# Far scores as one product of 256 columns, and weight splitting kept off GpSimd's copies

## The chip, the core and the metric

The kernel runs on one core of a Trainium2 chip. A core has five engines with instruction streams of their own: TensorE (PE, matrix products; its weight loads are shown as PEld), VectorE (DVE), ScalarE (ACT), GpSimd (POOL) and SyncE (SP, which issues the DMAs here). They share an on-chip memory of 128 partitions (SBUF); PE writes its products to a second, small memory (PSUM) of eight banks of 512 fp32 columns. The metric is the device time of one execution in microseconds, the median of the runs.

## The reference, cut to what matters

One block of a conformer: an input projection, a gated causal convolution branch, an attention branch, a merge by gates, and a feed-forward part. 1024 tokens, width 1024, 16 heads of 64. The attention is the sum of three dilated windows, mixed by their log-sum-exp:

```python
DILATION_GROUPS = ((128, 1), (512, 4), (2048, 16))
...
    scores = jnp.einsum('nbqhd,nbkhd->nbhqk', qb, kc)
...
    scores = scores - slopes[:, None, None] * dist
    scores = jnp.where(valid[None, :, None], scores, -jnp.inf)
    m = jnp.max(scores, axis=-1, keepdims=True)
    p = jnp.exp(scores - m)
...
        mix = jax.nn.softmax(jnp.stack(lses), axis=0)
        o = jnp.einsum('gbsh,gbshd->bshd', mix, jnp.stack(outs))
```

A softmax over three windows mixed by log-sum-exp is one softmax over the union, in which a key that lies in several windows counts as often. The kernel computes that: the mask holds the logarithm of the count less the slope times the distance.

## The kernel before, in words

All products are made with fp32r operands, each fp32 number split into a high part (rounded, `hi`) and a low part (`lo`, the rest). A product of two split operands is three matmuls: high by high, high by low, low by high. The splitting is work for ACT (the rounded copy) and DVE (`lo = src - hi`).

The attention loop (L1104 on) is written out by hand for ACT, DVE, PE and POOL: within `tc.manual_schedule` the instructions of these engines keep the order of the program. SP's DMAs are put in order by a planner. The loop has 128 slots, 8 places for each of the 16 heads, and 13 slots more in which the work still under way runs out (`BACK` = 12). For each head, places 0 to 3 score the query tiles 3, 2, 1, 0 of the first half of the tokens (128 queries against the keys up to them); place 4 scores `far`, the second half's queries against the first half's keys by residues of the position modulo 4; places 5 to 7 score the query tiles 7, 6, and 4 with 5 against the near keys.

A slot does this, in this order:

- `score` (L931): the products of queries and keys into PSUM, then on DVE `least` (L925), which adds the mask and takes the least of the negated sum. The queries are one operand with high and low part on alternating partitions; the keys come as `kh` and `kl`, and two products (L922 and L923) are added up in PSUM.
- `share` (L969), in places 1 to 4, for the unit scored one slot before: DVE's reciprocal, and on POOL the multiplication `times` (L967).
- `piece_high(2)` (L186), if more than two pieces wait in the deque: ACT rounds one half of a weight tile or of an activation tile (L190). The pieces belong to the filler products.
- `fill(front)`: filler, that is so many steps of the generator `side_steps`, each three matmuls of 512 columns (L118 to L120) of the gate projection or of the convolution's output projection. They are independent of the attention, and keep PE at work while the attention's chain passes through the other engines.
- `by_residue` (L917), in places 7, 0 and 1 (`COPIES`): on POOL, copies of the queries, of `kh` and of `kl` of the next or the present head into `fars`, ordered by residue.
- `flip` (L1006), for what was scored twelve slots ago: transposes on PE (into `pp`), the high part on ACT (`ph`, L1034) and the low part on DVE (`pl`, L1035). In places 0 to 3 this is the second half of the tokens, far, (4), (5) and (6, 7, 3); in places 4 to 6 the first half.
- `weigh` (L1040), for what was flipped one slot ago: the products with the values, first with `ph`, then with `pl`.
- `result`, `compare`, `combine`: in place 5 `compare` and in place 6 `combine` (L993) compute what share of the softmax the far and the near part of a query has. `combine` has POOL multiply eight tiles: four of `far`, then those of the tiles 7, 6, 4, 5.
- `powers` (L963): ACT's exponential of the unit scored in this slot.
- `o_step` (L1079), in the last slots: a sum, a rounded copy and a subtraction on the attention's output, for the projection that follows.
- `piece_low` (L180): the subtraction on DVE (L183) for what `piece_high` has rounded.
- `fill(behind)`, and `piece_high(2)` once more.

`FRONT` and `BEHIND` say how many filler steps stand in each place; the first four slots have one more each (`START`).

PSUM: the pool `psA` has two tiles of two banks (`big_ps`), `psB` four of one bank (`bank_ps`). The scores use one bank each; a tile of `psA` is taken for two scores in turn (`score_banks`). Ahead of the attention, `psA` holds the last gate products (`gx`), which are copied out at L880.

Of the kernel before, what the change touches and what calls it, by code (L numbers as in the profile page):

```python
# [21 lines left out]
P = 128  # L22
# [12 lines left out]
WARM = 7  # L35
FRONT = (1, 1, 1, 1, 0, 1, 1, 1)
BEHIND = (1, 0, 0, 0, 1, 0, 1, 0)
BACK = 12
COPIES = (-1, 0, 1)
START = (1, 1, 1, 1, 0, 0, 0, 0, 0, 0, 0, 0)  # L40
TAIL = (1, 1)
# [18 lines left out]
def block_kernel(ctx: ExitStack, tc: tile.TileContext, x, xT, x0, g2, pack, mask,  # L60
# [10 lines left out]
    def big_ps(name):  # L71
        return psA.tile([P, T], F32, tag="A", name=name)
# [823 lines left out]
    if True:  # L896
# [17 lines left out]

        fars = p2b.tile([P, 3, 512], F32R, name="fars")

        def by_residue(h, n):  # L917
            t = tiles[h][0][:, 512:] if n == 0 else tiles[h][n][:, 0:512]
            pool.tensor_copy(fars[:, n].rearrange("p (r j) -> p r j", r=4), t.rearrange("p (j r) -> p r j", r=4))

# [10 lines left out]
        def score(h, tiles, units):  # L931
            q, kh, kl, m = tiles
            made = []
            if not score_banks:
                pair = big_ps(f"s_{h}_{units[0]}")
                score_banks.extend((pair[:, 512:], pair[:, :512]))
            s = score_banks.pop()
            tag, size = ("pf", 512) if units == ("far",) else ("p" + "".join(map(str, units)),
                                                            sum((i + 1 - lowest(i)) * P for i in units))
            whole = ready2(tag, [P, size], F32, 2, f"{tag}_{h}")  # L940
            if units == ("far",):
                for r in range(4):
                    scored(s[:, r * P : (r + 1) * P], *(fars[:, n, r * P : (r + 1) * P] for n in range(3)))
                for r in range(4):
                    pt = whole[:, r * P : (r + 1) * P]
                    pts[h, "far", r] = pt, own[h][:, 1, r]
                    least(pt, s[:, r * P : (r + 1) * P], m[:, 512:640], own[h][:, 1, r, 0:1])
                    made.append(pts[h, "far", r])
                return made
            at = 0  # L950
            for i in units:
                ks = slice(lowest(i) * P, (i + 1) * P)
                c = slice(at, at + ks.stop - ks.start)
                at = c.stop
                scored(s[:, c], q[:, i * P : (i + 1) * P], kh[:, ks], kl[:, ks])
                st = own[h][:, 0, i - 4] if i > 3 else ready2("st", [P, 8], F32, 4, f"st_{h}_{i}")
                pts[h, i] = whole[:, c], st
                made.append((s[:, c], m[:, 512 - c.stop + c.start : 512], *pts[h, i]))
            for sc, mc, pt, st in made:
                least(pt, sc, mc, st[:, 0:1])  # L960
            return [u[2:] for u in made]

        def powers(pt, st):  # L963
# [136 lines left out]
        ENG = mybir.EngineType  # L1100
        with tc.manual_schedule(engines={ENG.Activation, ENG.DVE, ENG.PE, ENG.Pool}):
            pend = []
            fill(1)
            for at in range(len(slots) + BACK + 1):  # L1104
# [14 lines left out]
                for unit in late:  # L1119
                    share(*unit)  # L1120
                if len(pieces) > 2:
                    piece_high(2)
# [26 lines left out]
                if at == len(slots):  # L1149
# [3 lines left out]
                    heads = [o_fetch(0, k) for k in range(0, KT - 2, 2)]  # L1153
                if at > len(slots) + 3:
                    o_step(heads)
                if at == len(slots) + BACK - 4:
                    heads.append(o_fetch(0, KT - 2))
                piece_low()
                fill(behind)
                piece_high(2)  # L1160
            for _ in gates:
# [627 lines left out]
```

## Time and profile before

| | us |
|---|---|
| median of 3 runs | 1702.61 (1701.63 to 1704.5) |
| profiled execution, its own time | 1701.83 |
| span of its trace | 1699.4 |
| PE busy | 1685.3 (99%) |
| DVE busy | 1298.0 (76%) |
| ACT busy | 785.8 (46%) |
| POOL busy | 226.5 (13%) |

How to read the rows: in an answer of the timeline, the columns are the start in us from the start of the span, the duration in us, the engine, the line, the operation, output and inputs by the program's names, and the shape with the number of instructions merged into the row; in brackets stands how long the engine was idle before it and who released it. In a row of waits, the columns are the waiting engine and line, the releaser, the time waited in all, how often, and the longest. In a row of one line's or one tile's instructions, the three durations are the least, the median and the greatest in ns. Matmuls are pipelined: what a matmul costs is seen from the distance of two starts, not from its duration.

### The profile page before, as it was taken

Reading aid. Unit: us, or ns where it says so; the run is one execution under the profiler, and the core shown is the slowest. Engines: PE = TensorE matmul, PEld = TensorE weight load, DVE = VectorE, ACT = ScalarE, POOL = GpSimd, SP = SyncE. Lnnn points to the kernel's source line nnn. Section 1 sums busy time; section 2 is a strip of 40 time slices with the busy share of each in tenths; the row PEclk is TensorE's granted clock in tenths of the full one; section 3 lists DMA queues with packets and bytes.
Section 4 is the critical chain, followed back from the end, with each engine's and each line's share of the span. In section 5 each row is a group of like instructions: output and inputs, shape, how many; then the busy total and the mean of one; then the engine's idle time right before and its main releaser. Section 6 shows DMA issues by size and latency. Waiting matters only on the chain.

```text
span 1699.4 us, 22935 instructions
## 1 busy us (share of the span) xinstructions
PE 1685.3 (99%) x8003; PEld 1402.9 (83%) x8003; DVE 1298.0 (76%) x2098; ACT 785.8 (46%) x1351; POOL 226.5 (13%) x300
## 2 busy tenths in 40 slices
PE   9999999999999999999999999999999999999999
PEld 8888888888888888788878888888888888888887
DVE  5999999999876467766657654887777777889863
ACT  5411233233245477777745433554554445543431
POOL 0000132033000245545420000000000000000000
PEclk9999999999999999999999999999999999999999
DMA  9411145344545977777759594622222222498851
GB/s 375 151 50 50 50 137 164 121 137 137 189 169 194 312 234 244 242 224 225 214 181 346 197 336 143 235 87 87 74 87 87 85 77 79 150 376 308 288 174 50
DMA packets 186867, 300.21 MB, mean 177 GB/s; under 512 B 32000, under 2 KB 89984, under 8 KB 186240
## 3 DMA queue, kind: packets, MB, share of 16 engines
q1 hardware_dynamic: 185456, 294.43, 51.1%
q10 hardware_dynamic: 1296, 4.33, 0.6%
q8 instruction: 63, 1.03, 0.3%
q14 instruction: 52, 0.43, 0.1%
HBM read 214.67 MB, written 83.89 MB: 176 GB/s over the span
## 4 chain that ended last, share of the span: by engine, by line
PE 94%; DVE 2%; DMA 1%; ACT 1%; issue 1%; SPq 0%; POOL 0%; ACTq 0%; DVEq 0%; POOLq 0%
PE dx L1595 7%; PE xz L142 6%; PE xz L143 6%; PE xz L144 6%; PE dy L1595 5%; PE qkv L135 5%; PE qkv L137 5%; PE qkv L136 5%; PE y L142 2%; PE y L143 2%; PE y L144 2%; PE pp L1013 2%; PE wo L135 2%; PE wo L136 2%; PE wo L137 2%; PE o L1052 1%
## 5 line engine op out<-in xcount | busy, mean ns | idle before, releaser
L135 PE MATMUL qkv<-hi_qkv,hT 128*128 128x512 f32 x384 | 151.2, 395 | 0.0
L137 PE MATMUL qkv<-hi_qkv,hT 128*128 128x512 f32 x384 | 149.8, 391 | 0.0
L136 PE MATMUL qkv<-lo_qkv,hT 128*128 128x512 f32 x384 | 149.8, 391 | 0.0
L1498 DVE SCALAR_TENSOR_TENSOR u<-u,pk 128x1023 f32<-128x1023 f32 x88 | 112.3, 1278 | 1.2 <-ACT u L1496 0.9
L111 POOL TENSOR_TENSOR rs<-ss,mhalf 128x8 f32<-128x8 f32 x32 | 66.2, 2072 | 294.3 <-DVE ss L110 294.2
L1035 DVE TENSOR_TENSOR pl<-pp,ph 128x512 fp32r<-128x512 f32 (+1 forms) x95 | 59.0, 621 | 56.7 <-ACT ph L1034 56.1
L584 DVE SCALAR_TENSOR_TENSOR cacc<-csum,both,cacc 128x512 f32<-128x512 f32 x120 | 89.5, 746 | 0.3
L584 DVE SCALAR_TENSOR_TENSOR cacc<-apad,pk,cacc 128x512 f32<-128x512 f32 x120 | 88.5, 746 | 0.0
L87 DVE TENSOR_TENSOR lo_uv<-raw_uv,hi_uv 128x1024 fp32r<-128x1024 f32 x20 | 24.5, 1226 | 79.2 <-ACT hi_uv L86 79.2
L137 PEld LDWEIGHTS qkv<-hi_qkv,hT 128*128 128x128 f32 x384 | 72.1, 188 | 15.0
L584 DVE SCALAR_TENSOR_TENSOR codd<-apad,pk,codd 128x513 f32<-128x513 f32 x112 | 83.8, 749 | 0.7 <-ACT codd L577 0.7
L136 PEld LDWEIGHTS qkv<-lo_qkv,hT 128*128 128x128 f32 x384 | 72.2, 188 | 14.3
L135 PEld LDWEIGHTS qkv<-hi_qkv,hT 128*128 128x128 f32 x384 | 72.1, 188 | 14.2
L1034 ACT ACTIVATE ph<-pp 128x512 fp32r<-128x512 f32 (+1 forms) x95 | 51.4, 541 | 45.7 <-PE pp L1013 45.3
L142 PE MATMUL xz<-h2left,hi_uv 128*128 128x512 f32 x176 | 68.6, 390 | 0.0
L142 PE MATMUL xz<-blk_t,hi_s3g 128*128 128x512 f32 x176 | 68.6, 390 | 0.0
L144 PE MATMUL xz<-blk_t,lo_s3g 128*128 128x512 f32 x176 | 68.5, 389 | 0.0
L144 PE MATMUL xz<-h2left,lo_uv 128*128 128x512 f32 x176 | 68.5, 389 | 0.0
L143 PE MATMUL xz<-h2left,hi_uv 128*128 128x512 f32 x176 | 68.5, 389 | 0.0
L143 PE MATMUL xz<-blk_t,hi_s3g 128*128 128x512 f32 x176 | 68.5, 389 | 0.0
L1496 ACT ACTIVATE u<-u,pk 128x1024 f32<-128x1024 f32 x44 | 54.5, 1239 | 9.5 <-DVE u L1485 4.5
L926 DVE CUSTOM_DVE_ANT_0 p<-s,m 128x256 f32<-128x256 f32 (+3 forms) x105 | 48.9, 476 | 13.1 <-POOL pf L967 3.9
(486 smaller groups left out, 5095.8 us busy)
## 6 DMA issues: line engine op xcount, KB each, us to landing
wr<-w_down SPq DMA_DIRECT2D x45, 512.0 KB, 5.6
gr<-dff SPq DMA_DIRECT2D x62, 256.0 KB, 5.2
raw_qkv<-w_qkv SPq DMA_DIRECT2D x24, 512.0 KB, 5.1
dff<-u SPq DMA_DIRECT2D x22, 512.0 KB, 2.6
raw_uv<-w_up SPq DMA_DIRECT2D x21, 512.0 KB, 3.2
raw_ug<-w_up SPq DMA_DIRECT2D x20, 512.0 KB, 3.2
dv<-v SPq DMA_DIRECT2D x16, 512.0 KB, 2.9
q<-dq SPq DMA_DIRECT2D x32, 256.0 KB, 3.8
```

The source lines that it names most:

```text
L111: pool.tensor_tensor(out=dst, in0=tmp, in1=mhalf[:, : tmp.shape[1]], op=ALU.pow)
L135: pe.matmul(ps, ah, hi[:, k % 2, :], start=(k == 0), stop=False)
L136: pe.matmul(ps, ah, lo[:, k % 2, :], start=False, stop=False)
L137: pe.matmul(ps, al, hi[:, k % 2, :], start=False, stop=(k == KT - 1))
L142: pe.matmul(o, wh[:, k, :], bh[:, k, :], start=(start and k == 0), stop=False, skip_group_check=not start)
L143: pe.matmul(o, wh[:, k, :], bl[:, k, :], start=False, stop=False, skip_group_check=not start)
L144: end = pe.matmul(o, wl[:, k, :], bh[:, k, :], start=False, stop=(k == 3), skip_group_check=not start)
L584: dve.scalar_tensor_tensor(out=out_, in0=src[:, i : i + size], scalar=w(i), in1=out_, op0=ALU.mult, op1=ALU.add)
L1035: dve.tensor_tensor(out=runs(pl[:, c]), in0=order(pp[:, c]), in1=runs(ph[:, c]).bitcast(F32), op=ALU.subtract)
L1496: act.activation(acc, src, AF.Identity, bias=pk[:, C_FB + ci : C_FB + ci + 1], scale=w(2))
L1498: dve.scalar_tensor_tensor(out=acc[:, d:], in0=src[:, : T - d], scalar=w(2 - d), in1=acc[:, d:], op0=ALU.mult, op1=ALU.add)
L1595: pe.matmul(banks[n][:, cols], a[:, c], b[:, d], start=(start and i == 0 and m == 0), stop=(stop and i == nf - 1 and m == 2), skip_group_c ...
```

## The change

There are four edits.

- Far scores. The keys' high and low part of a residue lie side by side (`far_k`, 4 residues, 2 parts, 128 columns), so that one product of 256 columns takes the place of the two of 128 that were added up in PSUM. High and low scores then stand in separate columns of PSUM, a whole tile of `psA` a head. DVE adds the low scores and the mask into SBUF (one operation of 512 elements), and `least` takes the high scores and that sum.
- PSUM. The tiles 3, 2, 1, 0 take two tiles of `psA` at place 0, a bank each in turn; the units of places 5 to 7 take a tile each and use its first bank.
- Filler. `FRONT` and `BEHIND` are other tuples with the same sum: places 0 and 2 have no filler, place 1 has two in front, place 4 two behind. `piece_low` and `piece_high` run only for the places in `APART`, 2 to 6.
- The last slots. `o_step` is left out in the slots 6 and 7 after the last score, and runs in 4, 5 and 8 to 12.

```diff
-FRONT = (1, 1, 1, 1, 0, 1, 1, 1)
-BEHIND = (1, 0, 0, 0, 1, 0, 1, 0)
+FRONT = (0, 2, 0, 1, 0, 1, 1, 0)
+BEHIND = (0, 0, 0, 1, 2, 0, 1, 1)
+APART = (2, 3, 4, 5, 6)
...
-        fars = p2b.tile([P, 3, 512], F32R, name="fars")
+        far_q = p2b.tile([P, 512], F32R, name="far_q")
+        far_k = p2b.tile([P, 4, 2, P], F32R, name="far_k")
...
-            pool.tensor_copy(fars[:, n].rearrange("p (r j) -> p r j", r=4), t.rearrange("p (j r) -> p r j", r=4))
+            o = far_k[:, :, n - 1] if n else far_q.rearrange("p (r j) -> p r j", r=4)
+            pool.tensor_copy(o, t.rearrange("p (j r) -> p r j", r=4))
...
-            if not score_banks:
-                pair = big_ps(f"s_{h}_{units[0]}")
-                score_banks.extend((pair[:, 512:], pair[:, :512]))
-            s = score_banks.pop()
+            if units == ("far",):
+                return score_far(h, m)
+            if units[0] > 3:
+                score_banks.append(big_ps(f"s_{h}_{units[0]}")[:, 0:512])
+            elif not score_banks:
+                two = [big_ps(f"s_{h}_{units[0]}{i}") for i in range(2)]
+                score_banks.extend(two[i][:, cs] for cs in HALVES for i in range(2))
+            s = score_banks.pop(0)
...
+        def score_far(h, m):
+            s = big_ps(f"s_{h}_far").rearrange("p (r a j) -> p r a j", r=4, a=2)
+            whole = ready2("pf", [P, 512], F32, 2, f"pf_{h}").rearrange("p (r j) -> p r j", r=4)
+            for r in range(4):
+                pe.matmul(s[:, r].rearrange("p a j -> p (a j)"), far_q[:, r * P : (r + 1) * P],
+                          far_k[:, r].rearrange("p a j -> p (a j)"), start=True, stop=True)
+            dve.tensor_tensor(out=whole, in0=s[:, :, 1], in1=m[:, 512:640].unsqueeze(1).to_broadcast([P, 4, P]), op=ALU.add)
+            for r in range(4):
+                pts[h, "far", r] = whole[:, r], own[h][:, 1, r]
+                least(whole[:, r], s[:, r, 0], whole[:, r], own[h][:, 1, r, 0:1])
+            return [pts[h, "far", r] for r in range(4)]
...
+            apart = lambda at: at % 8 in APART or not 0 <= at < len(slots)
...
-                if len(pieces) > 2:
+                if len(pieces) > 2 and apart(at):
                     piece_high(2)
...
-                if at > len(slots) + 3:
+                if at - len(slots) in (4, 5, 8, 9, 10, 11, 12):
                     o_step(heads)
...
-                piece_low()
+                if apart(at):
+                    piece_low()
                 fill(behind)
-                piece_high(2)
+                if apart(at + 1):
+                    piece_high(2)
```

More of the change, by code (lines that the diff above doesn't have):

```diff
@@ L933, in score @@
             made = []
-            if not score_banks:
-                pair = big_ps(f"s_{h}_{units[0]}")
-                score_banks.extend((pair[:, 512:], pair[:, :512]))
-            s = score_banks.pop()
-            tag, size = ("pf", 512) if units == ("far",) else ("p" + "".join(map(str, units)),
-                                                            sum((i + 1 - lowest(i)) * P for i in units))
-            whole = ready2(tag, [P, size], F32, 2, f"{tag}_{h}")
[L941 to L949, printed above, removed]
+            if units == ("far",):
[6 more added lines that the diff above has]
+            s = score_banks.pop(0)
+            tag, size = "p" + "".join(map(str, units)), sum((i + 1 - lowest(i)) * P for i in units)
+            whole = ready2(tag, [P, size], F32, 2, f"{tag}_{h}")
             at = 0
```

## The prediction

> **What bounds the kernel now.** I read the page's first part and its chain first, then the stage that the change touches, which is the attention loop, from 570 to 885 us.
>
> ```profile
> span 1699.4 us, 22935 instructions
> PE 1685.3 (99%) x8003; PEld 1402.9 (83%) x8003; DVE 1298.0 (76%) x2098; ACT 785.8 (46%) x1351; POOL 226.5 (13%) x300
> PE 94%; DVE 2%; DMA 1%; ACT 1%; issue 1%; SPq 0%; POOL 0%; ACTq 0%; DVEq 0%; POOLq 0%
> 586.00:844.30 258.30, 250.76 (x1524) 215.20 (x1523) 175.26 (x623) 188.32 (x554) 133.05 (x218) 1.00 0.76 232
> ```
>
> TensorE (PE) is the bound and 94% of the chain that ends last. The last row (stretch; busy PE, PEld, DVE, ACT, POOL; clock; DMA share) runs from the first far product of head 0 to that of head 15: 15 heads in 258.3 us, 17.2 each, at the full granted clock. PE is idle in 7.5 us of it; no other engine is above 73%. So a gain is either PE work that goes, or a PE wait that goes.
>
> The waits of PE between 600 and 830 us, one of them followed through the engines, and the same operations undisturbed:
>
> ```profile
> PE s L922 <- DVE st L926: 3.4, 4, 1.1
> PE o L1052 <- DVE pl L1035: 2.7, 4, 0.8
> L183 DVE TENSOR_TENSOR aT<-raw_a,aT x16: 641/686/2533, 627.4 to 729.8; 128x512 fp32r<-128x512 f32 x16
> 715.76 1.10 POOL L919 CAST fars<-q 128x512 fp32r<-128x512 f32 x1
> 716.82 1.09 POOL L919 CAST fars<-kh 128x512 fp32r<-128x512 f32 x1
> 715.93 2.53 DVE L183 TENSOR_TENSOR aT<-raw_a,aT 128x512 fp32r<-128x512 f32 x1
> 718.93 0.67 DVE L1035 TENSOR_TENSOR pl<-pp,ph 128x512 fp32r<-128x512 f32 x1
> 718.40 0.48 PE L1051 MATMUL o<-ph,v 128*128 128x512 f32 x1
> 719.65 0.49 PE L1052 MATMUL o<-pl,v 128*128 128x512 f32 x1 [0.77 <-DVE pl L1035]
> 736.56 0.48 PE L1051 MATMUL o<-ph,v 128*128 128x512 f32 x1
> 736.87 0.39 PE L1052 MATMUL o<-pl,v 128*128 128x512 f32 x1
> 736.61 1.11 POOL L919 CAST fars<-kl 128x512 fp32r<-128x512 f32 x1
> 737.42 0.56 DVE L1035 TENSOR_TENSOR pl<-pp,ph 128x384 fp32r<-128x384 f32 x1 [0.94 <-ACT ph L1034]
> ```
>
> The subtraction of `piece_low` (L183, two SBUF operands) takes 0.69 us, but 2.53 where it meets two of GpSimd's (POOL's) copies: it ends 0.55 us after the second. Everything behind it on DVE is late, and PE waits for `pl`. The two products 719.65 and 718.40 stand 1.25 us apart; undisturbed they stand 0.31 apart (736.87 and 736.56), so a wait shown as 0.77 cost 0.94. The eight waits cost 6.1 + 8 x 0.17 = 7.5 us. On the lock, the Trainium skill, "SBUF — State Buffer", section "Who interferes with whom", says that a DVE instruction with two SBUF inputs contends with a GpSimd instruction that reads SBUF, and one with at most one such input does not. The trace agrees: `pl`, which reads PSUM and one SBUF tile, took 0.56 for 384 columns beside a copy (737.42) where it takes 0.67 for 512 without one.
>
> **The change, part by part.** One head of eight places, undisturbed on PE (728.98 is place 7, 730.65 place 0, 733.00 place 1, 735.33 place 2, 738.80 place 4):
>
> ```profile
> 728.98 0.39 PE L922 MATMUL s<-kh,q 128*128 128x256 f32 x1
> 729.32 0.28 PE L922 MATMUL s<-kh,q 128*128 128x256 f32 x1
> 729.44 0.28 PE L923 MATMUL s<-kl,q 128*128 128x256 f32 x1
> 729.56 0.40 PE L118 MATMUL ya<-aT,hi_co 128*128 128x512 f32 x1
> 730.25 0.28 PE L1051 MATMUL o<-ph,v 128*128 128x256 f32 x1
> 730.65 0.44 PE L922 MATMUL s<-kh,q 128*128 128x512 f32 x1
> 731.87 0.60 PE L1013 MATMUL pp_far<-ident,pf 128*128 128x128 f32 x4
> 733.00 0.34 PE L922 MATMUL s<-kh,q 128*128 128x384 f32 x1
> 734.05 0.60 PE L1013 MATMUL pp<-ident,p 128*128 128x128 f32 x4
> 735.33 0.33 PE L922 MATMUL s<-kh,q 128*128 128x256 f32 x1
> 736.31 0.49 PE L1013 MATMUL pp<-ident,p 128*128 128x128 f32 x3
> 738.80 0.22 PE L922 MATMUL s_far<-fars 128*128 128x128 f32 x1
> 739.64 0.62 PE L1013 MATMUL pp<-ident,p 128*128 128x128 f32 x4
> ```
>
> *1. The far products.* Eight products of 128 columns take 739.64 - 738.80 = 0.84 us, 0.11 each after the first. A product of 256 columns starts 0.12 us after the last one (729.32, 729.44, 729.56): twice the columns for the time of 128. Four take 0.48, so 0.36 x 16 heads = 5.8 us go. It all lies on PE, so it counts in full. The Trainium skill, "TensorE: Matmul & The Clock Gate", section "Back-to-back issue gap", gives 134 cycles for 128 columns and 262 for 256, by which the two forms cost the same; the rows disagree. Its section "LDWEIGHTS (loading the stationary operand)", columns over 1.2 GHz, some 107 ns as an estimate, agrees with the 0.11.
>
> *2. The subtractions kept off the copies.* If none of the eight waits comes back, 7.5 us go. The deque is small (40 pieces in 16 heads) and is worked off in five places as in eight; what moves is where.
>
> *3. The tail.* After the last slot, `o_step`'s sums of two SBUF operands hold up POOL, and PE with it:
>
> ```profile
> 870.52 1.22 DVE L1089 TENSOR_TENSOR raw_o<-raw_o,oT 128x1024 f32<-128x1024 f32 x1
> 869.70 4.19 POOL L967 TENSOR_SCALAR pf<-pf,both 128x128 f32<-128x128 f32 x4 [14.41 <-PE o L1052]
> 746.74 1.41 POOL L967 TENSOR_SCALAR pf<-pf,both 128x128 f32<-128x128 f32 x4 [5.32 <-DVE both L998]
> 870.74 0.40 PE L120 MATMUL ya<-aT,lo_co 128*128 128x512 f32 x1
> 874.03 0.48 PE L118 MATMUL ya<-aT,hi_co 128*128 128x512 f32 x1
> ```
>
> Four multiplications take 4.19 us against 1.41 in a quiet head. PE's next filler should start a third of a filler (0.23) and four transposes (0.36; three took 0.25 at 736.31) after 870.74, at 871.33; it starts at 874.03, 2.7 late. The steps of slots 6 and 7 after the last go, so this goes; but the two steps that they did are then made up in slots 8 to 10, two DVE operations of 1.2 us more there. I take 2.2, between 0.5 and 2.7.
>
> *4. What comes in return.* Fillers (0.70 us each: 729.56 to 730.25) leave places 0 (both) and 2 (its one) and go to 1, 3, 4; a head keeps ten. So places 0 and 2 lose cover:
>
> ```profile
> 730.00 1.74 POOL L967 TENSOR_SCALAR pf<-pf,both 128x128 f32<-128x128 f32 x4 [5.58 <-DVE both L998]
> 731.73 2.16 POOL L967 TENSOR_SCALAR p<-p,both 128x512 f32<-128x512 f32 x4
> ```
>
> Place 0: the far transposes come 0.70 earlier, at 731.17, the fourth at 731.50; POOL has it ready at 731.74: a wait of 0.3. In place 1 (1.40 earlier, less the 0.70 of its second filler, plus the 0.3) the second transpose comes at 733.76, POOL's eighth at 733.89: 0.2. A head with a subtraction in place 6 pays 0.5; counted by the code's own rule there are four. A quiet one has POOL 0.3 earlier and pays about 0.1; eleven. Sum 3.1. Bounds: 0 (the fillers lost were cover alone) and 0.7 a head, all of the cover, 10 in all.
>
> Place 2: `pp` comes 1.40 earlier, so DVE is through with `pl` at 737.98 - 1.40 = 736.6, just when the copy of `kl` runs (736.61 to 737.72, above). A subtraction there waits to 737.72 and ends 0.55 later, at 738.3, a second at 738.9. Then DVE has `least` and `pl` of place 3, 1.0 us (an estimate: 0.67, and under 0.3 for 128 columns at the same rate), and PE, with its far products at 738.80 - 0.70 = 738.1, wants that `pl` 0.48 + 0.36 + 0.2 later, at 739.1: a wait of 0.2 behind one subtraction, 0.8 behind two, or 0.3 where place 1 has already lost 0.5. By the code's rule six heads have one in place 2 and three have two: 6 x 0.2 + 3 x 0.6 (between 0.3 and 0.8) = 3.0, from 0 to 9 x 1.1 (a whole copy). The Trainium skill, "SBUF — State Buffer", the same section, says that issue order decides who blocks; the trace agrees (715.93 came 0.17 after a copy and lost), and by it a subtraction that comes first would delay the copy of `kl`, and the far products with it.
>
> Place 4: one sum more on DVE (512 elements from PSUM, like `pl` at 0.67), before four `least`. The filler added to this place is 0.70 of cover more, so the 0.67 is hidden; were that cover gone, 16 x 0.67 = 10.7. The sum's own inputs: one PSUM, one SBUF, like `pl`.
>
> PSUM: scores now take six two-bank tiles a head from the pool's two, where they took four. A score that opens a tile waits for the `least` of two places before (three before). The shortest such stretch, places 7 and 0, is 733.00 - 728.98 - 1.40 = 2.6 us long after the change, and `least` of 512 columns at `pl`'s rate 0.7: no price, up to 0.3 a head. At the start it has one:
>
> ```profile
> 580.81 0.33 PE L922 MATMUL s<-kh,q 128*128 128x384 f32 x1
> 581.01 0.60 ACT L880 ACTIVATE c<-gx 128x512 f32<-128x512 f32 x1 [9.21 <-PE gx L144]
> ```
>
> The second score of head 0 gets the tile that this last gate copy reads, and can't start before 581.6: 0.8 us, 0 if other work is put ahead, 1.5 if ACT is late.
>
> DMAs: none is added; SP's loads for the next head are asked for some 0.5 us a head earlier, and the DMA engines are 76% busy in the stretch, so I cost this at nothing.
>
> **The sum.** 5.8 + 7.5 + 2.2 = 15.5 go; 3.1 + 3.0 + 0.8 = 6.9 come; 8.6 less. The profiled execution took 1701.8 us (span 1699.4 and 2.4 around it), so 1693.2; the median of the runs, 1702.6, is 0.8 above it: 1694.0.
>
> **Rivals.** (a) *The cover holds everywhere*: DVE and POOL start their chains earlier too, because PE waits less. Nothing comes in return but the start: 1702.6 - 14.7 = 1688. For it: DVE is busy 68% of the stretch. Against it: the POOL rows end within 0.15 us of their users now. (b) *The waits only change place*: the copies, which POOL reaches late, meet the subtractions in place 2 instead (the change doesn't do what it says): parts 2 and 4 cancel but for 1, then 5.8 + 2.2 - 0.8 - 3.1 - 3.0 = 1.1 less, 1701.5. (c) *Slower: places 0 and 2 run dry.* POOL's eight multiplications set the head's pace if DVE's two-operand work holds POOL as in the tail (4.19 against 1.41, 2.8 late). From seven heads on it outweighs the 15.5 (7 x 2.8 = 19.6): 1702.6 - 15.5 + 3.0 + 0.8 + 19.6 = 1710. Against it: `piece_low` is out of places 7 and 0, where POOL multiplies. (d) *Columns alone set a product's price* and part 1 is nothing: 1694.0 + 5.8 = 1699.8. Against it stand the rows at 0.12. The Trainium skill's page on TensorE, as above, would have it so.
>
> **Chances.** The forecast, 4 to 12 us less: 0.50. (a) 0.18; (b) 0.15; (c) 0.12; (d) 0.05. A difference under 0.2% (3.4 us) can't be told from none. Below 1699.2: the forecast, (a), and the upper part of (b), 0.74. Within: the rest of (b), and (d), 0.14. Above 1706: (c), 0.12. The range, 1688 to 1702, leaves out (c) and the ends of (a).
>
> **What would show it.** Far products: four of 128x256, 0.48 us to the next. L183: a maximum near 1.8 us or less, no 2.5. PE waits for `pl` and `st`: fewer in places 1 to 3, new ones for POOL at `pp_far` and `pp`, for DVE at place 4. The tail's four multiplications near 1.4 us. Wrong: if PE's idle time in the loop is not below 7.5 us, step 4 is too small; if the 15 heads' stretch of 258.3 us does not come to about 258.3 - 5.4 - 7.5 + 6.1 = 251.5 (15 x 0.36 go), a term of steps 1, 2 or 4 is wrong, and which one the waits tell.

## The result, and the profile after

The changed kernel takes 1705.39 us (median of 22 runs, 1700.41 to 1707.47), the kernel before 1702.76 beside it (22 runs): a ratio of 1.0012, with a 95% interval from 1.0006 to 1.0019. That is within the 0.2% that the prediction called no change, on the slower side of it, and above the whole range that was forecast (1688 to 1702).

The first part and the chain of the page of after:

```profile
span 1705.2 us, 22809 instructions
PE 1682.5 (99%) x7939; PEld 1399.0 (82%) x7939; DVE 1298.9 (76%) x2114; ACT 787.7 (46%) x1351; POOL 223.8 (13%) x300
...
PE 89%; DMA 5%; ACT 2%; SPq 2%; DVE 1%; issue 1%; POOL 0%; ACTq 0%; DVEq 0%; POOLq 0%
```

PE has less to do than before (1682.5 against 1685.3) and yet the span is 5.8 us longer. (That is more than the 2.6 us between the medians: the profiled execution of after took 1707.0 us, that of before 1701.83.) In the chain PE's share fell from 94% to 89%, and what took its place is DMA (5%, it had 1%) and SP's queue (2%, it had none). The waits of PE between 600 and 830 us, in after, the same stretch that the prediction showed of before:

```profile
PE s L926 <- DMA kl<-dk: 6.9, 8, 2.2
PE o L1061 <- DVE pl L1044: 2.5, 4, 1.5
PE s L925 <- DMA kh<-dk: 2.1, 1, 2.1
PE o L1061 <- DVE pl_far L1044: 0.3, 1, 0.3
```

The waits for `st` on DVE have gone, and in their place stand nine waits for a head's keys, 9.0 us: loads that the kernel before, in the same stretch, never waited for. The stretch of the attention from the first far product to that of head 15 (columns as in the prediction's row of this view: stretch; busy PE, PEld, DVE, ACT, POOL; clock; DMA share; GB/s), in the windows of before:

```profile
586.03:843.80 257.77, 250.23 (x1520) 214.70 (x1518) 175.23 (x623) 187.79 (x553) 132.99 (x218) 1.00 0.76 232
```

The same in the windows of after:

```profile
587.57:848.65 261.08, 248.37 (x1459) 212.12 (x1458) 176.72 (x638) 189.53 (x552) 132.38 (x218) 0.99 0.75 228
```

And in the windows of e7, the changed kernel with fewer and larger loads that is described below:

```profile
585.99:834.47 248.48, 246.01 (x1459) 209.93 (x1458) 180.78 (x638) 189.45 (x552) 132.89 (x218) 1.00 0.80 241
```

After needs 3.3 us more for it than before, where 6.8 less were forecast. The share of the DMA engines (the number before the last) is nearly the same, 0.76 and 0.75, and in the last row, where the keys aren't late, it is higher. So the engines' share, over the stretch, does not say whether a load is late.

What does is the order on SP. SP's timeline of after, ahead of one of the waits:

```profile
697.48 4.04 SPq L994 DMA_DIRECT2D other<-own  x3
701.62 1.31 SPq L990 DMA_DIRECT2D other<-own  x2
703.04 0.54 SPq L154 DMA_DIRECT2D q<-dq  x1
703.67 1.19 SPq L1073 DMA_DIRECT2D do<-ot  x2
704.96 1.26 SPq L990 DMA_DIRECT2D other<-own  x2
706.31 0.55 SPq L154 DMA_DIRECT2D kh<-dk  x1
706.95 0.55 SPq L154 DMA_DIRECT2D kl<-dk  x1
707.55 0.59 SPq L154 DMA_DIRECT2D q<-dq  x1
708.19 0.59 SPq L154 DMA_DIRECT2D kh<-dk  x1
708.82 0.59 SPq L154 DMA_DIRECT2D kl<-dk  x1
```

And PE's timeline of after at the end of it:

```profile
710.05 0.40 PE L121 MATMUL ya<-aT,lo_co 128*128 128x512 f32 x1
712.51 0.47 PE L925 MATMUL s<-kh,q 128*128 128x512 f32 x1 [2.06 <-DMA kh<-dk]
713.51 0.47 PE L926 MATMUL s<-kl,q 128*128 128x512 f32 x1 [0.54 <-DMA kl<-dk]
713.82 0.60 PE L1022 MATMUL pp_far<-ident,pf 128*128 128x128 f32 x4
```

The chain of waits of after, at the same place:

```profile
708.19 0.59 SPq L154
708.82 4.56 DMA kl<-dk
713.51 0.47 PE s L926
```

SP issues one transfer after another, some 0.6 us each, with hardly a gap. The last load of `kl` is issued at 708.82, PE is through with its fillers at 710.45, and the load lands 4.56 us after its issue. In front of the loads stand `other<-own` (the exchange of `combine` and `compare`, eight transfers of 1 KB a head, L990 and L994) and `do<-ot` (the output's rows), which have to wait for other engines, and everything behind them waits too.

Worked out from SP's rows of the trace, between the far products of heads 1 and 14, per head (issuing: the sum of the durations, each at most 0.62; hand-over: the rest of the time, up to 0.1 between two; the waits: what goes beyond, put down to a semaphore that SP's own transfers use in turn, or to one of another engine; the transfers of after from 590 to 840 us signal eight semaphores in turn, each 40 or 41 times):

| kernel | a head | transfers | issuing | hand-over | waits, own eight | waits, engines |
|---|---|---|---|---|---|---|
| before | 17.6 us | 22.9 | 13.0 | 1.8 | 1.1 | 1.7 |
| after | 17.9 us | 22.8 | 13.0 | 1.8 | 1.4 | 1.7 |
| e7: after, one load for each of q, kh, kl | 17.0 us | 20.4 | 10.9 | 1.9 | 1.9 | 2.3 |
| e13: e7 with the mask in four transfers | 17.4 us | 23.0 | 12.1 | 1.8 | 3.2 | 0.3 |

In after 14.8 us of a head are SP's own work, 16.2 with the waits for one of its eight. PE of the changed kernel wants a quiet head every 16.6 us (below), and these heads take 17.0 on the average where no load is late (e7). The 0.4 to 0.8 us left are less than one long wait for `do<-ot` (two of its transfers take 3.25 us at 692.19), so by this sum the loads come later from head to head until PE waits for them. It is a circle, since SP's `do<-ot` waits for what PE finishes. This sum is an argument; that SP's queue is the bound is shown by the experiments.

### The profile page after: what moved, and what is told of

Same layout as the page of the kernel before. It is cut to its first block, busy times and chain, and to the rows that moved or that the text cites. A ratio compares the mean times of both kernels' runs of the same rounds, so it can differ in the third digit from the quotient of the medians.

```text
span 1705.2 us, 22809 instructions
## 1 busy us (share of the span) xinstructions
PE 1682.5 (99%) x7939; PEld 1399.0 (82%) x7939; DVE 1298.9 (76%) x2114; ACT 787.7 (46%) x1351; POOL 223.8 (13%) x300
## 4 chain that ended last, share of the span: by engine, by line
PE 89%; DMA 5%; ACT 2%; SPq 2%; DVE 1%; issue 1%; POOL 0%; ACTq 0%; DVEq 0%; POOLq 0%
PE dx L1607 7%; PE xz L143 6%; PE xz L145 6%; PE xz L144 6%; PE dy L1607 5%; PE qkv L136 5%; PE qkv L138 5%; PE qkv L137 5%; DMA kl<-dk 3%; PE y L145 2%; PE y L143 2%; PE y L144 2%; PE wo L138 2%; PE wo L136 2%; PE wo L137 2%; PE pp L1022 1%
## 5 line engine op out<-in xcount | busy, mean ns | idle before, releaser
L929 DVE CUSTOM_DVE_ANT_0 p<-s,m 128x512 f32<-128x512 f32 (+1 forms) x120 | 59.2, 503 | 33.3 <-PE pp_far L1022 11.4
```

The source lines that it names most:

```text
L929: dve.tensor_tensor_reduce(out=pt, in0=s, in1=m, scale=-1.0, scalar=3e38, op0=ALU.add, op1=ALU.min, accum_out=nm)
```

## The experiments

Theory S: SP's queue, worked off in order, is the bound that the freed time runs into (S' from e9 on: it is the number of transfers that counts, and one less can do). Against it: the loads are merely asked for too late (a matter of where they stand); the bytes and the DMA engines (B); or one of the parts of the change costs the time itself. Ratios are to the kernel before, run beside.

**e1. The loads asked for earlier.**

```diff
-                    if place == 1 and h + 1 < H:
+                    if place == 0 and h + 1 < H:
```

> The changed kernel, with the loads of the next head's q, kh, kl and mask asked for in place 0 instead of place 1, so that they stand ahead of the exchange of statistics in SP's queue. Theory S (SP's queue is late: the loads stand behind small transfers that wait, and PE waits for them at place 0): the nine waits of PE for kl and the one for kh (9.8 us shown in the changed kernel) go for the most part, and the two stretches of slow products behind them; 1690 to 1696 us. Theory B (the DMA engines are short of throughput, order does not matter): 1703 to 1707, the waits stay or move to other loads. Theory D (the new waits are DVE's and POOL's, as the prediction had it, and the loads only show up behind them): no change, 1705.

1699.31 us, 0.9978 [0.9969, 0.9987]. No wait for `kl` is left, but PE waits for `pl` ten times (7.2 us from 560 to 890 us), and in the trace it is `other<-own` that comes late to DVE instead (4.5 us in four waits). The place in the queue moves the wait from the loads to the exchange; it gives back 6 us and not 12, so there is more than a load put in the wrong place.

**e2. The exchange in two transfers instead of eight.**

```diff
-            for i in range(4):
-                sp.dma_start(other[h][32 * i : 32 * i + 32, 1], own[h][:, 0, i])
+            sp.dma_start(other[h][:, 1], own[h][:, 0])
...
-            for i in range(4):
-                sp.dma_start(other[h][:, 0, i], own[h][32 * i : 32 * i + 32, 1])
+            sp.dma_start(other[h][:, 0], own[h][:, 1])
```

> The changed kernel, with the exchange of statistics as two transfers a head instead of eight; the near and far parts then are compared by wrong rows, so the output is not the reference's. 8 KB a head either way, so no bytes go, but six issues of some 0.64 us each go from SP's queue. Theory S: SP has some 3.8 us a head more, the waits for kl and kh go, 1690 to 1696. Theory B: 1703 to 1707, since no bytes go. Theory D: 1705.

1692.46 us, 0.9936 [0.9923, 0.9948]. The waits of PE from 600 to 830 us, in this kernel:

```profile
PE o L1059 <- DVE pl L1042: 2.2, 4, 1.1
```

Six transfers a head less, the same 8 KB in two of 4 KB each, and all the waits for the keys are gone: 13 us. A head takes 17.0 us by the measure of the table. The edit also takes small packets from the DMA engines (those under 512 B fall from 32000 to 18176 on the page), but that is not what brings the keys in time: from the first far product to the last the engines' share is 0.78, above the 0.75 of after, and from 597 to 814 us the median load of `kl` takes 4.7 us from its issue to its landing, where it takes 4.2 in after. The loads don't land faster; they are issued earlier.

**e5. The same in the kernel before.**

```diff
-            for i in range(4):
-                sp.dma_start(other[h][32 * i : 32 * i + 32, 1], own[h][:, 0, i])
+            sp.dma_start(other[h][:, 1], own[h][:, 0])
...
```

> The control for the run with the short exchange: the kernel before, with two transfers for the exchange instead of eight (the output is not the reference's). Theory S (SP's queue is the limit only once PE is faster than some 17.8 us a head): the kernel before loses 1.0 us to kl, and the waits behind the copies stay, so 1699 to 1703; the change then is worth some 8 to 10 us between this and the changed kernel with the short exchange (1692.5). If SP's queue held the kernel before up as well, in ways that no wait shows: 1692 to 1696, and the change is worth nothing even without that limit.

1700.94 us, 0.9987 [0.9978, 0.9995]. The kernel before gains 1.5 to 2.2 us by it, no more: at its 17.6 us a head SP keeps up, but for the one wait for `kl` of 1.0 us. So with room on SP the change is worth 1700.9 - 1692.5 = 8.5 us.

**e3. The fillers, `APART` and the last slots alone**, without the far products and the PSUM tiles that go with them.

```diff
-FRONT = (1, 1, 1, 1, 0, 1, 1, 1)
-BEHIND = (1, 0, 0, 0, 1, 0, 1, 0)
+FRONT = (0, 2, 0, 1, 0, 1, 1, 0)
+BEHIND = (0, 0, 0, 1, 2, 0, 1, 1)
+APART = (2, 3, 4, 5, 6)
...
```

> The kernel before, with the new places of filler and subtractions and the new last slots, and the far scores and PSUM tiles as before. By the prediction's steps 2, 3 and 4: 7.5 + 2.2 less, some 5 us more, so 1698. Theory S: PE's pace is about 16.9 us a head, still faster than SP's 17.8, so part of the waits for kl come here too, 1700 to 1705. Theory B: the same as S.

1706.15 us, 1.0015 [1.0006, 1.0024]. PE's waits from 560 to 890 us:

```profile
PE s L923 <- DVE st L927: 6.9, 13, 0.9
PE o L1053 <- DVE pl L1036: 2.8, 3, 1.3
PE s L924 <- DMA kl<-dk: 0.7, 1, 0.7
```

Thirteen waits of a score for the `least` of the score before it: in the old use of PSUM the two scores of places 0 and 1 share a tile, and the program's order makes the second wait for the reader of the first. In before fillers stood between them. So the new tuples need the new use of PSUM; the one without the other is a loss. This run doesn't price the second step, since it makes a wait that neither kernel has.

**e4. The far products and the PSUM tiles alone**, `APART` all eight places.

```diff
+APART = (0, 1, 2, 3, 4, 5, 6, 7)
-        fars = p2b.tile([P, 3, 512], F32R, name="fars")
+        far_q = p2b.tile([P, 512], F32R, name="far_q")
+        far_k = p2b.tile([P, 4, 2, P], F32R, name="far_k")
...
```

> The kernel before, with the 256-column far products and the new PSUM tiles alone; filler, subtractions and last slots as before. By the prediction's step 1: 5.8 less, 0.8 more at the start: 1697.5. Theory S: the waits behind the copies still slow PE, so SP's loads come less late than in the changed kernel, but some do: 1698 to 1703. If the tighter use of PSUM or the sum on DVE costs: waits of PE for st or own of more than 5 us, 1703 to 1708.

1706.2 us, 1.0018 [1.0009, 1.0026]. The same 16 x 0.36 us of PE work are gone, and the first row of PE's waits (560 to 890 us) says where they went:

```profile
PE s L926 <- DMA kl<-dk: 6.2, 6, 2.3
```

Each half of the change alone is a loss, for two different reasons, and this one is that of the whole.

**e6. The mask loaded once**, for head 0, and used for all heads.

```diff
-            m = p2.tile([P, 640], F32, tag="m", bufs=2, name=f"m_{h}")
+            m = tiles[0][3] if h else p2.tile([P, 640], F32, tag="m", bufs=2, name=f"m_{h}")
...
-            sp.dma_start(m, mask[h])
+            if not h:
+                sp.dma_start(m, mask[h])
```

> The changed kernel, with the mask of head 0 loaded once and used for all heads (the output is not the reference's): 320 KB of some 2 MB a head go, and one issue of 0.6 us. Theory S (issues and their order): at most a sixth of what six issues gave, about 2 us, so 1702 to 1705. Theory B (bytes): a sixth of the loop's bytes go, with no exchange touched, and most of the waits with them: 1693 to 1698.

1693.79 us, 0.9942 [0.9929, 0.9956]. I had expected that one transfer of 22.8 is too few to matter; it is worth as much as six. That speaks for a threshold (SP is within 0.4 to 0.8 us a head of its limit, and one transfer is 0.6), or for the 320 KB. Two waits for `kl` are left, 1.2 us.

**e7. One load each for q, kh and kl.** In DRAM the rows of high and low part stand in turn, and the keys' are written twice in the projection, so that a head's tile is one transfer of 512 KB instead of two of 256.

```diff
-    dq = [[dr.tile([P, 4, T], F32R, name=f"dq{i}_{a}") for a in range(2)] for i in range(2)]
-    dk = [[dr.tile([P, 4, T], F32R, name=f"dk{i}_{a}") for a in range(2)] for i in range(2)]
+    dq = [dr.tile([2 * P, 4, T], F32R, name=f"dq{i}") for i in range(2)]
+    dk = [[dr.tile([2 * P, 4, T], F32R, name=f"dk{i}_{a}") for a in range(2)] for i in range(2)]
...
-            for s in range(2):
-                fetch(q[s:P:2, :], dq[g8][s][r : r + DH, hp % 4, :])
-                fetch(kh[s:P:2, :], dk[g8][0][r : r + DH, hp % 4, :])
-                fetch(kl[s:P:2, :], dk[g8][1][r : r + DH, hp % 4, :])
+            fetch(q, dq[g8][2 * r : 2 * r + P, hp % 4, :])
+            fetch(kh, dk[g8][0][2 * r : 2 * r + P, hp % 4, :])
+            fetch(kl, dk[g8][1][2 * r : 2 * r + P, hp % 4, :])
```

> The changed kernel, with q, kh and kl of a head in one transfer each instead of two: q's high and low rows lie interleaved in DRAM, and kh's and kl's rows are written there twice by the projection. The same bytes are loaded in the loop, in three issues less a head; 32 issues more stand in the projection, where SP has time. Theory S: half of what six issues less gave (13 us), or more since the loads themselves come earlier: 1694 to 1700. Theory B: 1704 to 1707.

1692.89 us, 0.9936 [0.9924, 0.9949]. All of the computation is kept, and this is the version that beats both kernels. A head's loads move the same bytes in three transfers fewer, and its PE waits from 600 to 830 us are one row, that of e2:

```profile
PE o L1061 <- DVE pl L1044: 2.2, 4, 1.1
```

So fewer bytes aren't needed; B falls as the only cause. Not all that SP gains here is number: the issues that are left are shorter too (the same mask 0.42 us by the median, where it is 0.58 in after).

**e8. e7 with the loads at place 0**, as in e1.

```diff
-                    if place == 1 and h + 1 < H:
+                    if place == 0 and h + 1 < H:
```

> The same with the loads asked for in place 0. Theory S: the waits for kl and kh gone, and the exchange no later than in the changed kernel, so the waits of the early loads alone for the exchange (DVE's comparison for other) shrink too: 1692 to 1697. Theory B: as the early loads alone, 1699 or more.

1693.73 us, 0.9941 [0.9929, 0.9954]: no different from e7. With room on SP the loads' place is worth nothing.

**e11. The control: the edit of e7 in the kernel before.**

```diff
-                fetch(q[s:P:2, :], dq[g8][s][r : r + DH, hp % 4, :])
...
+            fetch(q, dq[g8][2 * r : 2 * r + P, hp % 4, :])
...
```

> The kernel before, with q, kh and kl of a head loaded by one DMA each instead of two (their rows interleaved in DRAM, k written to both rows in the projection, so one stage has more to write); what is computed is unchanged. It is the control for the changed kernel with the same loads (1692.9). Theory S' (the change is worth 8 to 9 us wherever SP has room, and the kernel before has PE waits of its own, not SP's): 1700 to 1702. If the paired loads themselves were the gain, and the change worth nothing: 1693 to 1695.

1700.45 us, 0.9983 [0.9975, 0.9992]. The loads in one transfer are worth nearly 3 us by themselves, and the change, on top of them, 1700.45 - 1692.89 = 7.6.

**e9. The mask on ACT's queue.**

```diff
-            sp.dma_start(m, mask[h])
+            act.dma_start(m, mask[h])
```

> The changed kernel with one edit: a head's mask tile is asked for on ACT's queue instead of SP's; the same bytes move, and what is computed is unchanged. Theory S' (SP's queue, worked off in order at about 0.6 us a transfer, sets the head's pace): one issue less a head is worth 15 x 0.6 us of SP's time, and since without the mask SP has room for the 16.6 us head, the kernel takes 1692 to 1697 us and the wait for kl goes. Theory B (the 320 KB of the mask and the DMA engines' share are what makes kl late): nothing changes, 1704 to 1707. A middle value, 1698 to 1703, would mean that ACT's own issue, in front of its exponentials, costs what SP saves.

1702.3 us, 0.9996 [0.9987, 1.0004], in the middle. The wait for `kl` is gone but for 0.2 us, at the same bytes, as S has it; but ACT now stands still, by its timeline:

```profile
678.49 0.19 ACT L973 ACTIVATION_READ_ACCUMULATOR p<-p,st 128x1 f32 x1
681.43 0.34 ACTq L750 DMA_DIRECT2D m<-mask  x1
681.87 0.60 ACT L1043 ACTIVATE ph<-pp 128x512 fp32r<-128x512 f32 x1 [3.20 <-DMA other<-own]
```

The issue itself takes ACT 0.34 us. Ahead of it ACT waits 2.8 us for the semaphore that the mask's load is to signal; a transfer of the exchange that SP issued at 676.35 still has it. The eight are shared between the two queues, so ACT inherits SP's waits, ahead of the `ph` that PE needs.

**e10. The mask's first 8 columns in place of the mask**, after head 0.

```diff
+            else:
+                few_m = p2.tile([P, 8], F32, tag="fm", bufs=2, name=f"fm_{h}")
+                sp.dma_start(few_m, mask[h][:, 0:8])
```

> The changed kernel with the mask loaded whole for head 0 only (so the other heads are masked with that of head 0: a part of the computation is left out); in its place every further head asks for 8 columns of it into a tile of its own. SP issues as many transfers as before, with 316 KB a head less to move. Theory S' (number of issues): about as the changed kernel, 1701 to 1706. Theory B (bytes): about as with the mask loaded once, 1692 to 1696.

1700.22 us, 0.9986 [0.9977, 0.9995]. The run didn't test what it was made for. Nothing reads the small tiles, so nothing held their loads back, and all 15 were issued from 561 to 584 us, ahead of the first heads:

```profile
574.57 6.30 SPq L754 DMA_DIRECT2D fm<-mask  x7
...
609.87 0.47 PE L929 MATMUL s<-kh,q 128*128 128x512 f32 x1 [3.74 <-DMA kh<-dk]
```

What it shows is the queue by itself: seven of these transfers of 4 KB, with what they wait for, hold SP for 6.3 us, the keys of head 2 are 3.7 us late, and from far product to far product that head takes 23.2 us where it takes 16.0 in e6. That is about the difference between the two kernels (1700.2 and 1693.8).

**e13. e7 with the mask in four parts.** The same bytes, three transfers more.

```diff
-            sp.dma_start(m, mask[h])
+            for c in range(0, P, 32):
+                sp.dma_start(m[c : c + 32], mask[h][c : c + 32])
```

> The changed kernel with paired loads, and with the mask of a head loaded in four parts of 32 partitions instead of at once: the same bytes, three transfers more for SP to issue, 23.4 a head where the changed kernel has 22.8 and the paired one 20.4; what is computed is unchanged. Theory S' (the number of issues in SP's order sets the pace): the wait for kl and kh comes back and with it the time of the changed kernel or a little more, 1701 to 1708. If the paired loads gained by something else (the rows' order in DRAM, the bytes): no change, 1692 to 1694.

1696.05 us, 0.9964 [0.9950, 0.9978], 3.2 us above e7 (4.8 by the ratios), where S gave 8 or more. The wait for the keys is back (600 to 830 us):

```profile
PE s L927 <- DMA kl<-dk: 3.8, 3, 2.6
PE o L1062 <- DVE pl L1045: 1.2, 3, 0.4
...
```

With the same bytes, the number of transfers alone brings the wait back, which is what S says; its size was wrong. SP's own work is only 13.9 us a head here, less than the 14.8 of after, but the waits for one of its own eight semaphores have grown to 3.2 (the table's last row), and with them SP has 17.1 of the head's 17.4. So the issues by themselves don't decide it. One thing more differs from after: a head's keys are two transfers here, where in after five stand from the first `kh` to the last `kl`. The longest wait of this run is not one for a late issue but for a load which took 7 us to land (`kl` issued at 721.48, used at 728.64), with the four parts issued right behind it; the DMA engines' share was 1.05 from 725.0 to 728.7. There the engines may bear a part, which no run separates.

**e14. e11 with the far products and the PSUM tiles (e4) alone.**

```diff
+APART = (0, 1, 2, 3, 4, 5, 6, 7)
-        fars = p2b.tile([P, 3, 512], F32R, name="fars")
+        far_q = p2b.tile([P, 512], F32R, name="far_q")
+        far_k = p2b.tile([P, 4, 2, P], F32R, name="far_k")
...
```

> The kernel before with paired loads (1700.45) and of the change only the far products of 256 columns with the banks of PSUM that go with them; subtractions still stand in all places, the fillers and the output's steps as before. It prices the first step of the prediction, 5.8 us, with the start's 0.8 against it. If that step is right: 1695 to 1696. If the freed time is lost to the subtractions that meet GpSimd's copies, or the columns set a product's price: 1699 to 1701.

1695.4 us, 0.9955 [0.9943, 0.9968], against 0.9983 for e11: 0.0028 of 1702.7, that is 4.8 us. The same edit that lost 3 us in e4.

**e15. e7 with the subtractions allowed in all eight places.**

```diff
-APART = (2, 3, 4, 5, 6)
+APART = (0, 1, 2, 3, 4, 5, 6, 7)
```

> The changed kernel with paired loads, with the subtractions of the fillers' operands allowed in all eight places again, beside GpSimd's copies; the fillers' places stay as in the change. It prices the second step of the prediction, 7.5 us less against 3.0 that come back at place 2: if both are right, 1692.9 + 4.5 = 1697.5, between 1696 and 1701. If keeping the operands apart is worth nothing where SP has room: 1692 to 1694.

1694.5 us, 0.9955 [0.9943, 0.9968], 1.6 us above e7 by the medians and 3.2 by the ratios, whose intervals overlap; less than the 4.5 expected. Three of the five runs lie between 1693.8 and 1694.5 us, two at 1697.3 and 1697.5, and the trace is of the former of these two. In it no subtraction for `aT` is held up for 2.5 us, but one for the weights' low part `lo_co` is, and PE waits for the `pl` behind it:

```profile
L184 DVE TENSOR_TENSOR aT<-raw_a,aT x16: 637/686/1419, 626.9 to 727.9; 128x512 fp32r<-128x512 f32 x16
693.24 2.82 DVE L184 TENSOR_TENSOR lo_co<-raw_co,hi_co 128x512 fp32r<-128x512 f32 x1
697.25 0.50 PE L1061 MATMUL o<-pl,v 128*128 128x512 f32 x1 [1.56 <-DVE pl L1044]
```

That head takes 20.1 us, where it takes 17.4 in e7. For the rest the moved fillers alone bring the subtractions to other times than the copies: from 586 to 850 us four of 36 take over 1.0 us, where it is eight in before and ten in e7, there none over 2.04. So without `APART` the long lock came back once; what `APART` saves in the kernel before can't be read from leaving it out of the new one.

**e12. e7 with the steps of the last slots as before.**

```diff
-                if at - len(slots) in (4, 5, 8, 9, 10, 11, 12):
+                if at > len(slots) + 3:
```

> The changed kernel with paired loads, with the steps of the output's sums back at the slots behind the last head where the kernel before has them (every slot from the fourth on). It prices the third step of the prediction alone, 2.2 us. If that step stands: 1695 (1692.9 + 2.2). If the gain is given back by the sum that now stands ahead of the last subtractions and waits for its DMA (a wait of 1.35 us for pl at 883 us in the trace of after): 1692.5 to 1694.

1692.91 us, 0.9942 [0.9930, 0.9954], as e7 by the median (1.0 us above it by the ratios, whose intervals overlap). PE's waits from 834 to 900 us in e7:

```profile
PE o L1061 <- DVE pl L1044: 2.2, 2, 1.8
PE yb L119 <- DVE gg L1217: 1.5, 1, 1.5
```

The same in e12:

```profile
PE pp_far L1022 <- POOL pf L976: 1.5, 2, 1.0
PE yb L119 <- DVE gg L1217: 1.3, 1, 1.3
```

One wait has taken the place of the other. In e7 the sum that was put off has to wait 1.74 us for its DMA (`oT<-do`, 869.7 us) and stands ahead of the last `pl` on DVE.

## Why the prediction was wrong, point by point

*The failed step* is the last sentence of the costs: "DMAs: none is added; SP's loads for the next head are asked for some 0.5 us a head earlier, and the DMA engines are 76% busy in the stretch, so I cost this at nothing." The share of the DMA engines was the wrong row for it. In the kernel before SP was already occupied for 15.9 of a head's 17.6 us (13.0 + 1.8 + 1.1), besides its waits for engines. A change that makes a head shorter asks SP to do the same number of transfers in less time, and that has a price even where none is added. What it cost: 9.0 us of waits, and 1.7 us each more after the two longest (last section); with room on SP, 1705.4 - 1692.9 = 12.5 us go (the same loads give the kernel before 2.8). The prediction had said that PE's idle time in the loop, if not below 7.5 us, would mean that step 4 is too small; it is 261.08 - 248.37 = 12.7 in after, but the waits say that it was the loads. The rows to look at stood in the trace of before: SP's timeline, and a wait for `kl` in its last heads, at 835.80 us, which the prediction's stretch (600 to 830 us) left out:

```profile
PE s L923 <- DMA kl<-dk: 1.0, 1, 1.0
```

*Step 1, the far products*: as said. In the timeline of after, the four take 0.47 us to the next product:

```profile
587.57 0.63 PE L964 MATMUL s_far<-far_k,far_q 128*128 128x256 f32 x4
588.04 0.39 PE L119 MATMUL gate<-hT,hi_gt 128*128 128x512 f32 x1
```

0.48 was forecast. With the start's 0.8 (shown as 0.69, a wait for the gate copy `c`), 5.0 us were to come; e14 against e11 gave 4.8. A quiet head of after takes 16.6 us where one of before takes 17.0. The rival by which columns alone set the price is out.

*Step 2, the subtractions*: the mechanism is right and the maximum not quite:

```profile
L184 DVE TENSOR_TENSOR aT<-raw_a,aT x16: 641/681/2149, 629.0 to 736.8; 128x512 fp32r<-128x512 f32 x16
```

2.15 us is left of 2.53, where 1.8 or less was expected, but the waits for `st` are gone. The one of 2.15 us (at 736.78) is not governed by `APART`: when a filler needs an operand that is not split yet, its generator has it split on the spot (`one_piece`, L279), here in place 1, beside the copies. In that the change is less than its description says, by which the splitting runs in the places 2 to 6 only. No run prices this step by itself. Steps 2, 3 and 4 together are e7 against e14: 0.9955 - 0.9936 = 0.0019 of 1702.7, that is 3.2 us (2.5 by the medians; the intervals overlap), where 7.5 + 2.2 - 6.1 = 3.6 were forecast.

*Step 4, what comes in return*: too large. PE is idle for 248.48 - 246.01 = 2.5 us in e7's stretch, 7.5 in that of before; the forecast had 6.1 us come back. Among e7's waits from 600 to 830 us there is none for POOL, so the 3.1 us of places 0 and 1 did not come. Of its four waits for `pl`, three are of 0.4 us and stand some 1.6 us behind the start of the far products, behind two subtractions in place 2 that met the copy of `kl`, much as the forecast had it; the fourth stands behind the subtraction that `APART` doesn't govern:

```profile
728.73 2.04 DVE L184 TENSOR_TENSOR aT<-raw_a,aT 128x512 fp32r<-128x512 f32 x1 [0.47 <-ACT aT L191]
731.42 0.51 PE L1061 MATMUL o<-pl,v 128*128 128x512 f32 x1 [1.07 <-DVE pl L1044]
```

Together they are 2.2 us, where 3.0 were forecast for place 2. The stretch is 9.3 us shorter than before's where 6.8 were forecast (1.5 of it by the loads, by e11's stretch of 256.3).

*Step 3, the tail*: the lock has gone as forecast, POOL's four multiplications take 1.41 us:

```profile
874.57 1.41 POOL L976 TENSOR_SCALAR pf<-pf,both 128x128 f32<-128x128 f32 x4 [14.14 <-DVE both L1007]
...
883.24 1.23 DVE L1098 TENSOR_TENSOR raw_o<-raw_o,oT 128x1024 f32<-128x1024 f32 x1 [1.10 <-DMA oT<-do]
884.38 0.55 DVE L1044 TENSOR_TENSOR pl<-pp,ph 128x384 fp32r<-128x384 f32 x1
```

but no gain shows (e12), since the step made up later waits for its own DMA with `pl` behind it. The 2.2 us of this term should have been near its lower bound. The work behind the attention loses some more: a wait of 1.5 us for `gg` (e7's second row above) that was 0.2 before, which no step had; 1.1 of it stand in e11 too, so most of it comes with the loads and not with the change.

*The sum*: 8.6 us were forecast; with room on SP the change gave 8.5 (e2 against e5) and 7.6 (e7 against e11). That this agrees so well is partly luck. In the profiled executions of e7 and e11 the stretch of the 15 heads is 256.3 - 248.5 = 7.8 us shorter where 6.8 were forecast, PE's busy time in it falling by 3.5 us where 5.4 were forecast and its idle time by 4.3 where 1.4 were; the stretch begins no later (585.99 against 585.95) where the start's 0.8 was forecast; and what follows it takes 0.6 us longer, where the tail's 2.2 were to go. *The rivals*: none was the one that came. (b), at 1701.5, comes nearest to the measured time, but by another mechanism; (c) did not happen, the wait for POOL at `pp_far` is not among the rows of after.

What is shown: with room on SP, made in two ways and in both kernels (e2 and e5, e7 and e11), the waits for the keys go and the forecast gain comes. What stays open: how the cost on SP divides between the issues, the eight semaphores and the time that a load takes to land when others are close behind it; e13 shows that the number counts at the same bytes, and that it isn't all.

## What to carry to other kernels

Before costing a transfer at nothing, look at the queue that issues it, not at the share of the DMA engines: count the transfers of one round of the loop, take the issue time from its rows, and set the sum against the round's time after the change. Small transfers cost as much there as large ones (here eight of 1 KB were a third of the queue), and one that waits for an engine holds all behind it. When a good change brings nothing, give the suspected next bound some room in both kernels before taking the change out: here the same edit lost 3 us and gained 5.

## What the runs showed of the hardware that I had not expected

A wait of PE of about two microseconds costs more than its length. The windows of after, 3.2 us ahead of and behind the end of the wait shown above (the clock is the number after the busy times):

```profile
711.00:714.20 3.20, 1.15 (x7) 0.83 (x7) 0.00 (x0) 0.32 (x2) 3.20 (x6) 1.00 0.93 294
714.20:717.40 3.20, 3.20 (x12) 2.54 (x10) 1.85 (x6) 1.41 (x3) 1.68 (x3) 0.55 0.99 309
```

The granted clock is 0.55 for the next 3.2 us, in which the fillers start 0.43 us apart and not 0.23:

```profile
715.09 0.63 PE L120 MATMUL ya<-aT,hi_co 128*128 128x512 f32 x1
715.52 0.63 PE L121 MATMUL ya<-aT,lo_co 128*128 128x512 f32 x1
```

About 1.7 us are lost: from 714.53 to 717.94, 3.41 us, the clock is 0.50. The same followed the waits of 2.19 us in after, of 3.74 in e10 and 2.58 in e13; between 1.4 and 2.3 us both cases occur (the clock was 0.50 from 683.09 to 686.50 behind a wait of 1.43 us in e9, and 1.00 behind one of 1.60 in after). The Trainium skill, "TensorE: Matmul & The Clock Gate", section "HAM oscillation — how this bites in real kernels", gives the rule that there be no idle gaps of PE over some 3.4 us; here gaps of 2.1 us did it, so the measurement asks for shorter ones.

The issue of a transfer takes SP about 0.5 to 0.6 us in after, and its size does not set that: from 590 to 840 us the medians are 0.60 for the 1 KB of `other<-own`, 0.56 to 0.59 for 256 KB of `q`, `kh` or `kl`, and 0.49 for 512 KB of `v`. It isn't fixed for a transfer either: the same mask of 320 KB takes 0.58 in after and 0.42 in e7, and why is not shown. ACT issued the mask in 0.34 (the row in e9). The Trainium skill, "DMA: Bandwidth & Descriptors", section "Issuing engines are not separate DMA queues", calls the sequencer's time to initiate a DMA usually small beside the DMA itself. For one transfer the trace agrees (0.59 against 4.56 us to landing); for 22.8 a head it does not help, since issuing is 13.0 us of the head's 17.9.
